# Loads of the opening stage on three queues, and the first high rows ahead of the second weight cast

## The chip, the cores and the metric

The kernel runs on one core of a Trainium2 chip. The metric is the device time of one execution in microseconds (us). Engines are named as in the profile: PE is TensorE (matmuls; PEld are its weight loads), DVE is VectorE, ACT is ScalarE, POOL is GpSimd, and SP is SyncE, which here only issues DMA transfers. A name with a q (SPq, ACTq, POOLq) is the queue of that engine, on which DMA issues and other instructions without data work stand.

## The reference

Two decoder layers over 256 tokens of width 1024, all in float32. What matters here is the first sub-layer's entry:

```python
mod = jax.nn.silu(c) @ w_ada + b_ada                 # c: (1, 1024), w_ada: (1024, 6144)
sh1, sc1, gt1, sh2, sc2, gt2 = jnp.split(mod, 6, axis=-1)
h = rms_norm(x, g_mix) * (1 + sc1[:, None, :]) + sh1[:, None, :]
proj = h @ w_in                                      # then two kinds of attention, gates, w_out
```

The layer then mixes the two attentions, adds the result to x, and runs a channel sub-layer (w_up, squared ReLU, w_down) behind a second norm of the same kind. Positions enter through rotary embedding of queries and keys.

## The kernel before

**Arithmetic.** Each float32 weight piece is split in two float32r parts, high and low: ACT casts the high part (`split_next`, L440) and DVE subtracts it for the low part (L446, or L961 in the opening stage). The activations are split the same way. A product is three matmuls (high by high, low by high, high by low).

**The opening stage** is `lead` (L881 to L1039). It is written out by hand: inside it each engine's instructions stand in exactly the order of the code, so a late instruction holds all that follow on its engine. Its order is as follows.

- `load_x` (L122) issues c and the two halves of x on SP, and on ACT's queue the positions, the rotary frequencies (`invf`) and the identity matrix (`ident`), the last two being columns of one tile, `cpack`. ACT's instructions wait behind these issues in its own order.
- `load_ada` loads four of sixteen pieces of the first w_ada columns; `ada_load` (L210) issues each piece as two transfers of 256 KB on SP. The four pieces of the first call, 0 to 3, hold the eight k rows of the shift and scale columns of the first two feature blocks, which is the first quarter, q = 0. Behind them stand the loads of w_in (`stream.load_next`, L418), then the next pieces.
- `silu_c` computes silu(c) on ACT and DVE. `load_rows` (L130) issues three small loads on ACT's queue behind it: the norm gains and the biases, as rows of one tile, `grow`. `rope_angles` (L343) puts some twenty small operations on DVE, which need the positions and `invf`.
- PE runs 24 wake matmuls on a tile of ones (L908).
- For each half t of x: ACT squares and sums (L926), DVE adds the two sums (L927), and POOL takes the power -1/2 (L928). POOL's earlier instructions are a few memsets. Between t = 0 and t = 1 stand the first two of eight weighted sums of the first quarter on DVE (`dve_sums`, L307, L313 and L315).
- ACT scales the rows of x by that power (`rows_scale`, L935), PE transposes them (L559, with `ident`), ACT copies the result (L939). PE transposes `grow` (L945), ACT copies it (`gcol`), PE runs eight more wakes. Then the second half of the columns: ACT scales both t (L935), PE transposes, DVE copies (L939), behind the last six weighted sums. PE turns the sums into columns (`columns`, L335).
- The quarter then passes the affine step (`apply`, L963): DVE adds biases and gains for shift `sh` and scale `s1` (L301, L304), ACT writes the high rows `hT_hi` of two feature blocks (L970, two instructions), DVE a full copy (L972) and the low rows (L975).
- Three casts of weights (`cast`, L956, which is `split_next` without the low part) serve the three groups of the product with w_in: queries, keys, values of the second attention (L977 on). In the kernel before two of the casts stand ahead of the first `apply`.
- The loop over q = 0 to 3 (L995) runs the product on PE quarter by quarter (`part`, L980, matmuls L984): the high by high matmuls of the three groups, then those with low parts. In between, PE sums the next quarter of w_ada (`pe_sums`, L325; for the last one DVE does it), `apply` prepares the next two feature blocks, and `cast` and `low` prepare the next weights. The 3 raw buffers of weights are refilled as they are read.

Eight semaphores take turns over the transfers of SP and ACT, so an issue also waits until an earlier transfer on its semaphore has landed; in the trace this shows as waits of SP's queue on transfers that have nothing to do with its own.

After the opening stage come the rest of the layer's product, attention, the mixing, the channel sub-layer and the second layer. None of their code is touched.

Of the kernel before, what the change touches and what calls it, by code (L numbers as in the profile page):

```python
# [15 lines left out]
P = 128  # L16
# [4 lines left out]
KT = D // P  # L21
HD = 64
HALF = HD // 2
# [55 lines left out]
def kernel(ctx: ExitStack, tc: tile.TileContext, io):  # L79
# [3 lines left out]
    nc = tc.nc  # L83
# [12 lines left out]
    def nm(s):  # L96
        cnt[s] = cnt.get(s, 0) + 1
        return f"{s}_{cnt[s]}"
# [7 lines left out]
    def ring(n, name):  # L106
        return work.tile([P, 512], F32, tag="ring", name=nm(name), bufs=RING)[:, :n]
# [3 lines left out]
    pos_i = const.tile([P, NT], I32, name="pos_i")  # L111
    cpack = const.tile([P, HALF + P + 4 * P], F32, name="cpack")
    invf = cpack[:, 0:HALF]
    ident = cpack[:, HALF:HALF + P]
    mask = cpack[:, HALF + P:]
    grow = ring(P, "grow")
# [5 lines left out]
    def load_x():  # L122
        nc.sync.dma_start(c8, io["c"][0].rearrange("(p k) -> p k", k=KT))
        for t in range(NT):
            nc.sync.dma_start(x_sb[:, t, :], io["x"][0, t * P:(t + 1) * P, :])
        nc.scalar.dma_start(pos_i, io["positions"][0].rearrange("(t p) -> p t", p=P))
        nc.scalar.dma_start(invf, io["cpack"][:, 0:HALF])
        nc.scalar.dma_start(ident, io["cpack"][:, HALF:HALF + P])

    def load_rows():  # L130
        nc.scalar.dma_start(grow[0:4 * KT, :], io["grow"])
        for l in range(DEPTH):
            o = (4 + 6 * l) * KT
            nc.scalar.dma_start(grow[o:o + 6 * KT, :], io["b_ada"][l].rearrange("(r c) -> r c", c=P))

    def load_gains():
        nc.sync.dma_start(gqk, io["gqk"][None].to_broadcast([P, DEPTH, 4, HD]))
# [20 lines left out]
    def silu_c():  # L158
        nc.scalar.activation(cs, ones[:, :KT], AF.Tanh)
        nc.scalar.activation(cs, c8, AF.Tanh, scale=0.5)  # L160
        nc.vector.scalar_tensor_tensor(out=cs, in0=cs, scalar=1.0, in1=c8, op0=ALU.add, op1=ALU.mult)
        nc.vector.tensor_scalar(out=cs, in0=cs, scalar1=0.5, scalar2=None, op0=ALU.mult)
        nc.vector.tensor_copy(cz[:, :, 0], cs)
# [46 lines left out]
    def ada_load(i):  # L210

        u, q = divmod(i, 4)
        if u >= len(ada_units) or i in ada_raw:
            return
        l, part, half = ada_units[u]
        col = part * D + half * 512
        src = io["w_ada"][l].rearrange("(p k) c -> p k c", k=KT)
        tag, o = room[i] if i < len(room) and room[i] else ("araw", 0)
        if tag == "araw":
            ada_raw[i] = araw.tile([P, 2, 512], F32, tag=tag, name=nm(tag))  # L220
        elif tag == "gt":
            ada_raw[i] = state.tile([P, D], F32, tag=tag, name=nm(tag), bufs=2).rearrange("p (k c) -> p k c", c=512)
        else:
            if o == 0:
                first[tag] = state.tile([P, 2, 2, 512], F32, tag=tag, name=nm(tag), bufs=1)
            ada_raw[i] = first[tag][:, o]
        if u < 4:
            for k in range(2):
                nc.sync.dma_start(
                    ada_raw[i][:, k, :].rearrange("p (a c) -> p a c", a=2),  # L230
                    src[:, 2 * q + k, 0:2 * D].rearrange("p (a c) -> p a c", a=2)[:, :, half * 256:half * 256 + 256])
        else:
            nc.sync.dma_start(ada_raw[i], src[:, 2 * q:2 * q + 2, col:col + 512])
# [8 lines left out]
    def ada_unit(u):  # L242
# [4 lines left out]
        for q in range(4):  # L247
            for a in range(ADA_BUFS if u > 3 else 0):
                ada_load(4 * u + q + a)
            raw = ada_raw[4 * u + q]  # L250
            if q == 2:
                bias_row(u + 1)
            for k in range(2):
                kk = 2 * q + k
                if kk == 0 and kind < 2:
                    nc.vector.tensor_scalar(out=acc, in0=raw[:, k, :], scalar1=cs[:, kk:kk + 1], scalar2=None,
                                            op0=ALU.mult)
                else:
                    nc.vector.scalar_tensor_tensor(  # L259
                        out=acc, in0=raw[:, k, :], scalar=cs[:, kk:kk + 1], in1=(bz if kk == 0 else acc),  # L260
                        op0=ALU.mult, op1=ALU.add)
                yield
# [34 lines left out]
    def ada_affine(l, sub, half, cols, n, kinds):  # L297
        for i, kind in enumerate(kinds):
            d = (sh if kind == 0 else s1)[l][sub][:, half * n:half * n + n]
            b = (4 + 6 * l + 3 * sub + kind) * KT + half * n  # L300
            nc.vector.tensor_tensor(out=d, in0=cols[:, i * n:i * n + n], in1=gcol[:, b:b + n], op=ALU.add)  # L301
            if kind == 1:
                g = (2 * l + sub) * KT + half * n
                nc.vector.scalar_tensor_tensor(out=d, in0=d, scalar=1.0, in1=gcol[:, g:g + n],  # L304
                                               op0=ALU.add, op1=ALU.mult)
# [25 lines left out]
    def columns(rows):  # L331

        ps = tmp_t()
        for i in range(4):
            nc.tensor.matmul(ps[:, i:i + 1], lhsT=rows[:, i * P:(i + 1) * P], rhs=ones[:, 0:1], start=True, stop=True,  # L335
                             skip_group_check=True)
        return ps
# [5 lines left out]
    def rope_angles():  # L343
        nc.vector.tensor_copy(pos_f, pos_i)
        ang = ring(NT * HALF, "ang").rearrange("p (t i) -> p t i", i=HALF)
        for t in range(NT):
            nc.vector.tensor_scalar(out=ang[:, t, :], in0=invf, scalar1=pos_f[:, t:t + 1], scalar2=None, op0=ALU.mult)
        ns = [ring(NT * HALF, "rtn").rearrange("p (t i) -> p t i", i=HALF) for _ in range(2)]
        for i in range(2):
            nc.vector.tensor_scalar(out=ns[i], in0=ang, scalar1=1.0 / (2.0 * math.pi), scalar2=0.25 * i,  # L350
                                    op0=ALU.mult, op1=ALU.add)
        for m in (MAGIC, -MAGIC):
            for i in range(2):
                nc.vector.tensor_scalar(out=ns[i], in0=ns[i], scalar1=m, scalar2=None, op0=ALU.add)
        for j, p in enumerate(TWO_PI_PARTS):
            for i in range(2):
                nc.vector.scalar_tensor_tensor(out=sincos[:, i], in0=ns[i], scalar=-p,
                                               in1=(ang if j == 0 else sincos[:, i]), op0=ALU.mult, op1=ALU.add)
        nc.vector.tensor_scalar(out=sincos[:, 1], in0=sincos[:, 1], scalar1=0.5 * math.pi, scalar2=None, op0=ALU.add)
        lim = 3.1415925  # L360
        nc.vector.tensor_scalar(out=sincos, in0=sincos, scalar1=lim, scalar2=-lim, op0=ALU.min, op1=ALU.max)
# [519 lines left out]
    def lead():  # L881
# [6 lines left out]
        def load_ada():  # L888
            for _ in range(4):
                ada_load(next(pieces))  # L890

        load_x()
        load_ada()
        stream.load_next()
        stream.between = load_ada
# [2 lines left out]
        load_ada()  # L898
        load_gains()
        silu_c()  # L900
        load_rows()
        rope_angles()

        wake_ps = tmp_t()
# [10 lines left out]
        r = [small.tile([P, 1], F32, tag="lnr", name=nm("lnr"), bufs=2) for _ in range(NT)]  # L915
# [38 lines left out]
        cols = columns(acc)  # L954

        def cast():  # L956
            stream.split_next("later")
# [5 lines left out]
        def apply(q, cols):  # L963

            ada_affine(0, 0, q, cols, 2, (0, 1))
            x = xnT[:, 2 * q:2 * q + 2, :]
            hf = ring(512, "hf").rearrange("p (j s) -> p j s", s=S)
            for i in range(2):
                j = 2 * q + i
                A.activation(hT_hi[:, j, :], x[:, i, :], AF.Identity, bias=sh[0][0][:, j:j + 1],  # L970
                             scale=s1[0][0][:, j:j + 1])
                V.tensor_scalar(out=hf[:, i, :], in0=x[:, i, :], scalar1=s1[0][0][:, j:j + 1],  # L972
                                scalar2=sh[0][0][:, j:j + 1], op0=ALU.mult, op1=ALU.add)
            js = slice(2 * q, 2 * q + 2)
            V.tensor_tensor(out=hT_lo[:, js, :], in0=hf, in1=hT_hi[:, js, :].bitcast(F32), op=ALU.subtract)  # L975
# [10 lines left out]


        cast()
        cast()
        apply(0, cols)  # L990
        cast()
        rope_sin()
        for _ in range(3):
# [1 line left out]
        for q in range(4):  # L995
# [21 lines left out]
            cols = columns(acc)  # L1017
# [23 lines left out]
    def mixing(l, rest, finish):  # L1041
# [6 lines left out]
        if l == 0:  # L1048
            with tc.manual_schedule():
                (qb, kb, vb), tabs = lead()  # L1050
        else:
            stream.retire(["qT", "kv"])
            tabs = rope_tables(l)
            qb = proj_first(rest, finish)
# [218 lines left out]
```

## Time and profile before

| | us |
|---|---|
| median of 3 runs | 757.29 (754.62 to 758.05) |
| profiled execution | 755.65 |
| its span in the trace | 753.9 |
| PE busy | 730.7 (97%) |
| DVE busy | 587.2 (78%) |
| ACT busy | 431.2 (57%) |
| POOL busy | 32.0 (4%) |

The span runs from the first to the last instruction; the rest of the execution's time lies around it. A row of a timeline gives the start, the duration, the engine, the line, the operation with output and inputs, how many instructions were merged (x8), and in brackets how long the engine had been idle and what released it. A row on a queue (ACTq) is the issue of a transfer, not the transfer. A chain of waits follows the end of the kernel back from each instruction to what released it. In time windows, busy times are us within the stretch, PEclk is the granted clock of TensorE as a share of full speed, and DMA is the mean busy share of the 16 DMA engines.

### The profile page before, as it was taken

Reading aid. Unit: us, or ns where it says so; the run is one execution under the profiler, and the core shown is the slowest. Engines: PE = TensorE matmul, PEld = TensorE weight load, DVE = VectorE, ACT = ScalarE, POOL = GpSimd, SP = SyncE. Lnnn points to the kernel's source line nnn. Section 1 sums busy time; section 2 is a strip of 40 time slices with the busy share of each in tenths; the row PEclk is TensorE's granted clock in tenths of the full one; section 3 lists DMA queues with packets and bytes.
Section 4 is the critical chain, followed back from the end, with each engine's and each line's share of the span. In section 5 each row is a group of like instructions: output and inputs, shape, how many; then the busy total and the mean of one; then the engine's idle time right before and its main releaser. Section 6 shows DMA issues by size and latency. Waiting matters only on the chain.

```text
span 753.9 us, 12320 instructions
## 1 busy us (share of the span) xinstructions
PE 730.7 (97%) x4713; PEld 645.3 (86%) x4713; DVE 587.2 (78%) x1090; ACT 431.2 (57%) x817; POOL 32.0 (4%) x24
## 2 busy tenths in 40 slices
PE   7999889999999999999999999999999999999997
PEld 6678778899778999989977888989988899999896
DVE  6598998999899988988789788987879745545542
ACT  6545579863466655455436357576447755555550
POOL 1003200000000000000000401000000000000000
PEclk9999999999999999999999999999999999999999
DMA  8996758877949999989882633844662865565501
GB/s 293 392 325 227 227 162 285 274 254 248 303 128 330 370 347 299 332 309 342 283 318 98 224 119 113 263 157 166 225 223 80 269 203 175 182 207 172 189 33 57
DMA packets 110538, 173.46 MB, mean 230 GB/s; under 512 B 4744, under 2 KB 68488, under 8 KB 110480
## 3 DMA queue, kind: packets, MB, share of 16 engines
q1 hardware_dynamic: 109744, 172.54, 67.9%
q8 instruction: 37, 0.61, 0.3%
q10 hardware_dynamic: 736, 0.15, 0.1%
q14 instruction: 21, 0.17, 0.1%
HBM read 171.62 MB, written 1.05 MB: 229 GB/s over the span
## 4 chain that ended last, share of the span: by engine, by line
PE 72%; DVE 13%; DMA 7%; ACT 3%; issue 2%; POOL 2%; SPq 0%; ACTq 0%; DVEq 0%; POOLq 0%
PE tmp L527 11%; PE acc L524 11%; PE acc L522 11%; PE acc L523 11%; PE tmp L528 10%; PE tmp L529 10%; DMA araw<-in_w_ada_dram 4%; DVE ada L259 2%; DVE w L446 2%; PE acc L984 2%; POOL rs L751 1%; ACT w L440 1%; PE tmp L870 1%; DMA wraw<-in_w_up_dram 1%; PE acc L810 1%
## 5 line engine op out<-in xcount | busy, mean ns | idle before, releaser
L446 DVE TENSOR_TENSOR w<-wraw,w 128x1024 fp32r<-128x1024 f32 x137 | 166.3, 1221 | 48.1 <-ACT w L440 46.8
L440 ACT CAST w<-wraw 128x1024 fp32r<-128x1024 f32 x150 | 155.9, 1048 | 78.9 <-PE acc L524 44.5
L527 PE MATMUL tmp<-hT_hi,w 128*128 128x256 f32 x480 | 140.1, 292 | 1.3 <-DVE alo L874 1.2
L529 PE MATMUL tmp<-hT_hi,w 128*128 128x256 f32 x480 | 135.9, 283 | 0.0
L528 PE MATMUL tmp<-hT_lo,w 128*128 128x256 f32 x480 | 135.7, 283 | 0.0
L259 DVE SCALAR_TENSOR_TENSOR ada<-araw,cs,ada 128x512 f32<-128x512 f32 x140 | 104.4, 746 | 3.2 <-DMA araw<-in_w_ada_dram 2.1
L527 PEld LDWEIGHTS tmp<-hT_hi,w 128*128 128x128 f32 x480 | 91.5, 191 | 8.2 <-issue 4.4
L528 PEld LDWEIGHTS tmp<-hT_lo,w 128*128 128x128 f32 x480 | 91.7, 191 | 0.7
L529 PEld LDWEIGHTS tmp<-hT_hi,w 128*128 128x128 f32 x480 | 91.6, 191 | 0.3 <-issue 0.3
L522 PE MATMUL acc<-w,uhi 128*128 128x512 f32 x192 | 75.4, 393 | 0.0
L523 PE MATMUL acc<-w,uhi 128*128 128x512 f32 x192 | 74.9, 390 | 0.0
L524 PE MATMUL acc<-w,ulo 128*128 128x512 f32 x192 | 74.9, 390 | 0.0
L1164 ACT ACTIVATE relu<-tmp 128x256 f32<-128x256 f32 x56 | 21.5, 384 | 68.8 <-PE tmp L529 68.8
L524 PEld LDWEIGHTS acc<-w,ulo 128*128 128x128 f32 x192 | 36.1, 188 | 7.6
L522 PEld LDWEIGHTS acc<-w,uhi 128*128 128x128 f32 x192 | 36.1, 188 | 6.9
L523 PEld LDWEIGHTS acc<-w,uhi 128*128 128x128 f32 x192 | 36.1, 188 | 6.8
L440 ACT CAST kv<-wraw 128x1024 fp32r<-128x1024 f32 x21 | 22.1, 1051 | 24.6 <-PE acc L524 19.8
L446 DVE TENSOR_TENSOR ahi<-wraw,ahi 128x1024 fp32r<-128x1024 f32 x18 | 22.0, 1222 | 15.0 <-ACT ahi L440 14.9
L446 DVE TENSOR_TENSOR kv<-wraw,kv 128x1024 fp32r<-128x1024 f32 x21 | 25.7, 1222 | 9.9 <-ACT kv L440 9.8
L446 DVE TENSOR_TENSOR qT<-wraw,qT 128x1024 fp32r<-128x1024 f32 x21 | 25.6, 1220 | 8.3 <-ACT qT L440 8.3
L527 PE MATMUL tmp<-hT_hi,alo 128*128 128x256 f32 x112 | 31.8, 284 | 0.0
L528 PE MATMUL tmp<-hT_lo,alo 128*128 128x256 f32 x112 | 31.7, 283 | 0.0
(248 smaller groups left out, 1744.8 us busy)
## 6 DMA issues: line engine op xcount, KB each, us to landing
araw<-in_w_ada_dram SPq DMA_DIRECT2D x80, 512.0 KB, 5.9
wraw<-in_w_up_dram SPq DMA_DIRECT2D x32, 1024.0 KB, 5.9
wraw<-in_w_down_dram SPq DMA_DIRECT2D x32, 1024.0 KB, 5.9
wraw<-in_w_in_dram SPq DMA_DIRECT2D x28, 1024.0 KB, 5.7
wraw<-in_w_out_dram SPq DMA_DIRECT2D x8, 1024.0 KB, 5.6
wraw<-in_w_in_dram SPq DMA_DIRECT2D x12, 512.0 KB, 7.1
wraw<-in_w_o_swa_dram SPq DMA_DIRECT2D x8, 512.0 KB, 3.3
wraw<-in_w_o_moba_dram SPq DMA_DIRECT2D x8, 512.0 KB, 5.1
```

The lines of the kernel that those rows point to most:

```text
L259: nc.vector.scalar_tensor_tensor(out=acc, in0=raw[:, k, :], scalar=cs[:, kk:kk + 1], in1=(bz if kk == 0 else acc), op0=ALU.mult, op1=ALU.add)
L440: nc.scalar.copy(hi, r)
L446: ins = nc.vector.tensor_tensor(out=lo, in0=r, in1=hi.bitcast(F32), op=ALU.subtract)
L522: nc.tensor.matmul(ps, lhsT=lh, rhs=rh, start=start, stop=False)
L523: nc.tensor.matmul(ps, lhsT=lh, rhs=rl, start=False, stop=False)
L524: nc.tensor.matmul(ps, lhsT=ll, rhs=rh, start=False, stop=stop)
L527: nc.tensor.matmul(ps, lhsT=wh, rhs=ah, start=start, stop=False)
L528: nc.tensor.matmul(ps, lhsT=wh, rhs=al, start=False, stop=False)
L529: nc.tensor.matmul(ps, lhsT=wl, rhs=ah, start=False, stop=stop)
L751: nc.gpsimd.tensor_tensor(out=rs, in0=ss, in1=mhalf[:, :NT * nh].rearrange("p (t h) -> p t h", h=nh), op=ALU.pow)
L984: T.matmul(ps[t], lhsT=left[:, 2 * q + k, t * P:(t + 1) * P], rhs=w[:, k, :], start=(first and k == 0), stop=(last and k == 1))
L1164: nc.scalar.activation(r, ps, AF.Relu)
```

## The change

Three edits, all in the opening stage. The pieces 1 and 3 of the first quarter of w_ada, two transfers each, are issued on ACT's queue instead of SP's, where they stand first in ACT's order. The six small loads (positions, frequencies, identity, and the three of `load_rows`) are issued on POOL's queue instead of ACT's, and `load_rows` is called right behind `load_x`, so that all six stand ahead of POOL's first power; the memsets stay ahead of them. And the first `apply` stands behind one cast of weights instead of two.

```diff
         for t in range(NT):
             nc.sync.dma_start(x_sb[:, t, :], io["x"][0, t * P:(t + 1) * P, :])
-        nc.scalar.dma_start(pos_i, io["positions"][0].rearrange("(t p) -> p t", p=P))
-        nc.scalar.dma_start(invf, io["cpack"][:, 0:HALF])
-        nc.scalar.dma_start(ident, io["cpack"][:, HALF:HALF + P])
+        nc.gpsimd.dma_start(pos_i, io["positions"][0].rearrange("(t p) -> p t", p=P))
+        nc.gpsimd.dma_start(invf, io["cpack"][:, 0:HALF])
+        nc.gpsimd.dma_start(ident, io["cpack"][:, HALF:HALF + P])
 
     def load_rows():
-        nc.scalar.dma_start(grow[0:4 * KT, :], io["grow"])
+        nc.gpsimd.dma_start(grow[0:4 * KT, :], io["grow"])
         for l in range(DEPTH):
             o = (4 + 6 * l) * KT
-            nc.scalar.dma_start(grow[o:o + 6 * KT, :], io["b_ada"][l].rearrange("(r c) -> r c", c=P))
+            nc.gpsimd.dma_start(grow[o:o + 6 * KT, :], io["b_ada"][l].rearrange("(r c) -> r c", c=P))
...
             for k in range(2):
-                nc.sync.dma_start(
+                (nc.scalar if i in (1, 3) else nc.sync).dma_start(
                     ada_raw[i][:, k, :].rearrange("p (a c) -> p a c", a=2),
...
         load_x()
+        load_rows()
         load_ada()
...
         silu_c()
-        load_rows()
         rope_angles()
...
         cast()
+        apply(0, cols)
         cast()
-        apply(0, cols)
         cast()
```

## Rows read from the trace of the kernel before

**Rows 1.** Time windows, last stretch; columns: busy us of each engine, granted clock, DMA.

```profile
60.40:753.90 693.50, 676.55 (x4425) 602.52 (x4423) 543.93 (x996) 397.84 (x766) 29.16 (x14) 1.00 0.66 221
```

**Rows 2.** Chain of waits in order of time, 0 to 60 us; columns: start, us, what.

```profile
7.66 5.03 DMA araw<-in_w_ada_dram
...
12.78 0.76 DVE aq L315
...
16.64 0.17 DVE s L304
```

**Rows 3.** Timeline of ACT, 0 to 45 us; columns: start, us, what, idle before and releaser.

```profile
3.78 0.34 ACTq L131 DMA_DIRECT2D grow<-in_grow_dram  x1
...
5.24 0.63 ACT L926 ACTIVATE ln<-x_sb 128x512 f32<-128x512 f32 x1 [1.26 <-DMA x_sb<-in_x_dram]
...
11.15 0.72 ACT L935 ACTIVATE ln<-x_sb,lnr 128x512 f32<-128x512 f32 x1 [1.21 <-POOL lnr L928]
...
13.31 1.35 ACT L935 ACTIVATE ln<-x_sb,lnr 128x512 f32<-128x512 f32 x2
...
15.41 1.04 ACT L440 CAST w<-wraw 128x1024 fp32r<-128x1024 f32 x1 [0.75 <-DMA wraw<-in_w_in_dram]
16.69 1.04 ACT L440 CAST w<-wraw 128x1024 fp32r<-128x1024 f32 x1 [0.24 <-DMA wraw<-in_w_in_dram]
17.64 1.09 ACT L970 ACTIVATE hT_hi<-ln,sh,s 128x256 fp32r<-128x256 f32 x2
...
35.57 1.05 ACT L440 CAST w<-wraw 128x1024 fp32r<-128x1024 f32 x1 [4.29 <-DMA wraw<-in_w_in_dram]
```

**Rows 4.** Timeline of PE, 0 to 58 us.

```profile
0.99 8.40 PE L908 MATMUL tmp<-ones 128*128 128x128 f32 x48 [0.99 <-POOL mhalf L148]
...
18.29 2.15 PE L984 MATMUL acc<-w,hT_hi 128*128 128x512 f32 x8 [2.02 <-ACT hT_hi L970]
20.27 1.07 PE L984 MATMUL tmp<-w,hT_hi 128*128 128x512 f32 x4
...
42.56 2.14 PE L984 MATMUL acc<-w,hT_hi 128*128 128x512 f32 x8 [1.14 <-ACT hT_hi L970]
```

**Rows 5.** Timeline of DVE, 0 to 20 us.

```profile
5.49 0.39 DVE L347 TENSOR_SCALAR ang<-cpack,pos_f 128x32 f32<-128x32 f32 x2 [0.76 <-DMA cpack<-in_cpack_dram]
...
8.04 0.23 DVE L361 TENSOR_SCALAR sincos<-sincos 128x128 f32<-128x128 f32 x1
...
16.38 0.16 DVE L301 TENSOR_TENSOR sh<-tmp,gcol 128x2 f32<-128x2 f32 x1
```

**Rows 6.** Timeline of POOL, 0 to 62 us.

```profile
1.38 0.31 POOL L156 MEMSET cz<- 128x256 f32 x1
8.54 0.65 POOL L928 TENSOR_TENSOR lnr<-lnr,mhalf 128x1 f32<-128x1 f32 x1 [6.84 <-DVE lnr L927]
10.12 0.99 POOL L928 TENSOR_TENSOR lnr<-lnr,mhalf 128x1 f32<-128x1 f32 x1 [0.93 <-DVE lnr L927]
```

**Rows 7.** All instructions of line 928; columns: count, min/median/max ns, first and last start.

```profile
L928 POOLq MODIFY_POOL_CONFIG  x2: 11/11/11, 1.6 to 1.7; - x2
L928 POOL TENSOR_TENSOR lnr<-lnr,mhalf x2: 654/824/995, 8.5 to 10.1; 128x1 f32<-128x1 f32 x2
```

**Rows 8.** DMA issues, 0 to 62 us: the small cpack load of ACT's queue.

```profile
cpack<-in_cpack_dram ACTq DMA_DIRECT2D x1, 16.0 KB, 4.2
```

**Rows 9.** Waits of SP's queue, 0 to 62 us; columns: us in total, times, longest.

```profile
SPq L229 <- DMA cpack<-in_cpack_dram: 3.3, 2, 2.9
```

**Rows 10.** Time windows of all engines, two stretches of loads.

```profile
6.50:13.50 7.00, 5.12 (x42) 4.70 (x42) 5.97 (x20) 4.20 (x12) 1.65 (x2) 1.00 0.92 287
...
20.00:48.00 28.00, 26.75 (x138) 18.75 (x138) 19.77 (x40) 13.56 (x18) 0.00 (x0) 1.00 1.07 390
```

**Rows 11.** Time windows of line 908 alone (wake matmuls), two single microseconds.

```profile
3.00:4.00 1.00, 1.00 (x7) 1.00 (x6) 1.00 0.92 361
8.00:9.00 1.00, 1.00 (x11) 1.00 (x10) 1.00 0.97 335
```

## The prediction

> **What bounds the kernel now.** I read the time windows first. From 60.4 us to the end PE is busy 676.55 of 693.50 us [rows 1]: none of the moved instructions lies there, and there is little idle time in which a late start could vanish. So the change acts in the first 60 us, and what the product with w_in gains or loses there reaches the end almost one for one. The chain of waits tells what comes before that product: a w_ada transfer is awaited until 12.69, the last three weighted sums run from 12.78 to about 15.1, and the scale s of the first two feature blocks is done at 16.81 (16.64 + 0.17) [rows 2]. The timeline of ACT shows the rest [rows 3]: the high rows (L970) start at 17.64 and not right behind s, because the second weight cast (16.69 to 17.73, itself behind its transfer) stands ahead of them. PE then starts at 18.29 after 2.02 us idle, begins its third group at 20.27, and waits once more for high rows, 1.14 us, ahead of 42.56 [rows 4]. DVE's table of angles (rope_angles) runs from 5.49, when its frequencies land, to 8.27, ahead of all sums; the affine step starts at 16.38 [rows 5].
>
> **POOL's queue, which I hold to decide.** Today POOL clears its last tile by 1.69 and then does nothing until its first power (L928) at 8.54 [rows 6]. But line 928 also shows two MODIFY_POOL_CONFIG at 1.6 and 1.7, 11 ns each [rows 7]: the power needs something set up, and the 6.85 us up to 8.54 hide whatever that takes, while POOL is listed as waiting for DVE. In the changed kernel six loads (positions, frequencies, identity, three of the grow rows) stand in POOL's queue in program order ahead of line 928. No row shows a load issued by POOL. From below an issue costs 0.34 us, the shortest on ACT's queue [rows 3]; from above 0.99, the longer of line 928's two one-element powers; I take 0.82, the middle of the two [rows 7], because both are work of POOL on almost no data. Six are 4.94 us (2.0 to 6.0): the configuration passes at 6.63 instead of 1.69. What it takes then is bounded by 0 and 6.85 us; I take the upper end, since that stretch is the only one in the trace in which it ran at all, and nothing on POOL begins inside it. The first power then starts at 13.48 and takes 0.65, and the second ends at 13.48 + 0.65 + 0.99 = 15.12, instead of 11.11 (10.12 + 0.99) [rows 6]: 4.01 us late. The Trainium skill (GPSIMD Engine Reference, 2.1 Instruction dispatch) says that the first call of a freshly loaded POOL kernel pays about 6 us, measured as 5.95 from MODIFY_POOL_CONFIG, with no visible instruction. By that figure the sum below would be 0.9 us lower; the trace of before fits it, with 6.85 us of room, and does not show it.
>
> **What follows from the late power.** The second scaling of rows (L935) starts 0.04 us after it, at 15.16 instead of 11.15 [rows 3]. From there to the end of L935's last pair (13.31 + 1.35 = 14.66) ACT and PE work in turn on each other's results, 3.51 us, and to the affine step (16.38) another 1.72 [rows 3, 5]: transposes, copies, column sums. So the pair ends at 18.67, the affine step starts at 20.39, and s is there at 20.82. The sums on DVE are done before they are needed: the frequencies, second on POOL, are issued at 2.51 and land 4.2 us later, as they do today [rows 8]; the table ends 2.78 us after that, by 9.5, and eight sums of at most 0.76 us end at 15.6, four microseconds ahead of the column sums. If that cover is gone, they bind: second rival.
>
> **The high rows ahead of the second cast.** ACT does the first cast behind the last scaling, 18.67 to 19.75, and the high rows right behind s at 20.85. The first matmul follows 0.65 later as today, at 21.50, which is 3.2 us late. But the order only exchanges: the second and third cast now stand behind 1.09 us of high rows and take 2 x 1.04 us [rows 3], so the third group starts at 20.85 + 1.09 + 2.08 + 0.03 = 24.05 instead of 20.27. PE's order is fixed, so 3.78 us is what the product is late. Taken alone, the edit gives the first group 0.83 us (17.64 - 16.81) and takes most of it back at the third.
>
> **Loads.** SP loses four issues and the 3.3 us for which its w_ada issues wait on the cpack loads of ACT's queue [rows 9]. ACT gets four issues for six, each 0.3 to 0.5 us, and the four all stand ahead of its table load: that and the tanh move by some tenths, hidden by the 1.26 us for which ACT waits for x today [rows 3]; without that wait the tenths would count. The new loads share the DMA engines with x, so x lands later, by at most the 1 MB put beside it, 2.7 us at 390 GB/s: ACT's squares would start at 7.9 instead of 5.24 and still have 5.6 us until the first power. Identity and grow rows are read by PE after 14.9, later than today, and POOL has issued all six by 6.63. From 6.5 to 13.5 the DMA engines move 287 GB/s, and 390 later [rows 10]: with a fuller queue that stretch gives back up to 7 x (1 - 287/390) = 1.8 us, and all of w_in's loads come up to that much sooner. On the path this is worth the following: ACT's cast at 35.57 waits 4.29 us for its transfer [rows 3], DVE's low part, tables and sums come behind it, and the 1.14 us idle of PE ahead of 42.56 is their end. With the transfers sooner and PE 3.8 us later that idle time goes; next late there is PE itself, busy to 41.42.
>
> **Sum.** 3.78 - 1.14 = 2.64 us late. The profiled execution took 755.65 us (span 753.9, the rest around it), so 758.3; it lies 1.64 under the median of the runs, 757.29, so against that 759.9. Bounds: issues at 0.34 or 0.99 us move it by -2.9 or +1.0, the configuration by down to -6.85, until other things bind (second rival).
>
> **Rivals.** First, slower: TensorE's clock falls. Today the longest idle stretch of PE that a row shows is the 2.02 us, and every window is granted 1.00, that is 2.4 GHz. In the forecast PE has nothing between its wake matmuls (end 9.39) [rows 4] and its first transposes, at 14.9 (first power done at 14.13, then 0.04 and 0.72 for ACT's scaling): 5.5 us. The wakes ran 7 to a microsecond from 3 to 4 us and 11 from 8 to 9 [rows 11], though both rows say 1.00; I read the first rate as the level of 1.2 GHz. If the clock falls in the gap and the next 6 us of work (the first rise lay between 4 and 8 us) run at that rate, it costs 6 x (1 - 7/11) = 2.2 us: +4.8 us, 762.1. It decides as soon as POOL is late enough for the gap; against it speaks that transposes, second wakes and column sums come before the product and take part of the slow time where PE waits anyway. The Trainium skill (TensorE: Matmul & The Clock Gate, Part 1) says that an idle array goes back to half its clock; no idle stretch of before is long enough to agree or not. Second, the configuration costs nothing that shows, or does not stand behind the loads: then the sums on DVE bind, 15.6 instead of 15.1, s is there at 17.3, the third group starts at 17.33 + 3.2 = 20.53, 0.3 late, and with the 1.14 us back it is 0.8 faster: 756.5. Third, POOL's small loads also land no later than today and the w_ada loads sooner: sums from 8.27 without a wait end at 14.4, s is there at 16.1, the third group at 19.3, 1.0 sooner, and with the 1.14 it is 2.1 faster: 755.2. Against it speaks that x and the first pair of w_ada share the engines with what ACT issues before them.
>
> **How the numbers follow.** 0.5% is 3.8 us, about what a measurement of this kernel can tell from no change. Forecast 0.42, first rival 0.28, second 0.18, third 0.12. Slower by over 0.5%: nearly all of the first rival and the forecast's upper end (+3.7 at 0.99 us an issue), 0.32. Faster by over 0.5% would need 3.8 us, more than the third rival has: 0.04 for what I do not see. The rest, 0.64, is no change. The range goes from 755.4, just above the third rival, to 764.0, the first rival with issues of 0.99 us (763.1) and a microsecond for the runs.
>
> **What would show it.** Line 928: configuration behind six issues of POOL at about 6.6, first power near 13.5, second scaling near 15.2. High rows near 20.9 with one cast ahead, first product matmul near 21.5, third group near 24. No idle PE where the 1.14 us were. The SP waits on cpack gone, 6.5 to 13.5 us above 287 GB/s. A first power before 9 us is the second or third rival; a granted clock under 1.00, or matmuls of twice the length, ahead of the third group is the first. A time under 755 us would mean that I have missed what the loads held up.

## The result, and the profile after

| | before | after |
|---|---|---|
| median of the runs, us | 756.89 (754.62 to 758.05) | 765.79 (765.36 to 766.32) |
| profiled execution, its span, us | 755.65, 753.9 | 765.57, 763.8 |
| mean granted clock of the profiled execution | 1.000 | 0.987 |

The ratio is 1.0117, interval 1.0091 to 1.0143: slower by 8.9 us, or 1.2%. A second set of runs (last experiment) gave 1.0086 (1.0060 to 1.0113), 6.3 us: a loss of 6 to 9 us. The forecast was 759.9 us, no change, with 764.0 as its upper end.

The timeline of ACT, 0 to 30 us, of the changed kernel (columns as in [rows 3]):

```profile
0.74 0.99 ACTq L229 DMA_DIRECT2D araw<-in_w_ada_dram  x2
2.93 4.62 ACTq L229 DMA_DIRECT2D ahi<-in_w_ada_dram  x2
7.58 1.28 ACT L159 ACT_TABLE_LOAD   x1 [7.58 <-DMA x_sb<-in_x_dram]
...
9.11 0.21 ACT L160 ACTIVATE cs<-c 128x8 f32<-128x8 f32 x1
9.23 0.61 ACT L926 ACTIVATE ln<-x_sb 128x512 f32<-128x512 f32 x1
...
15.42 0.72 ACT L935 ACTIVATE ln<-x_sb,lnr 128x512 f32<-128x512 f32 x1 [0.84 <-POOL lnr L928]
...
19.27 1.05 ACT L440 CAST w<-wraw 128x1024 fp32r<-128x1024 f32 x1
23.05 1.09 ACT L970 ACTIVATE hT_hi<-ln,sh,s 128x256 fp32r<-128x256 f32 x2 [2.73 <-DVE s L304]
24.05 1.98 ACT L440 CAST w<-wraw 128x1024 fp32r<-128x1024 f32 x2
```

Read the first three rows as one. The two issues of piece 1 take 0.99 us. The two of piece 3 take 4.62 us, and ACT's first instruction of any work, the table load, follows them at 7.58 with x named as what ended the wait. Each issue by itself is short (0.37 us in the trace); the second of this pair stood until 7.17, when the second half of x had landed. The squares (L926), at 5.24 before [rows 3], start at 9.23, and the high rows (L970) at 23.05 instead of 17.64.

The timeline of DVE, 0 to 24 us:

```profile
9.36 0.17 DVE L161 SCALAR_TENSOR_TENSOR cs<-cs,c 128x8 f32<-128x8 f32 x1 [9.36 <-DMA ahi<-in_w_ada_dram]
...
10.11 0.39 DVE L347 TENSOR_SCALAR ang<-cpack,pos_f 128x32 f32<-128x32 f32 x2
...
12.79 0.21 DVE L927 TENSOR_SCALAR lnr<-lnv 128x1 f32<-128x1 f32 x1
12.92 0.47 DVE L313 TENSOR_SCALAR aq<-araw,cs 128x512 f32<-128x512 f32 x1
...
21.24 1.29 DVE L939 COPY ln<-tmp 128x512 f32<-128x512 f32 x2 [2.34 <-PE tmp L559]
22.54 0.16 DVE L301 TENSOR_TENSOR sh<-tmp,gcol 128x2 f32<-128x2 f32 x1
```

The first row names a w_ada transfer as its releaser, but cs waits for the tanh, which ends at 9.32 on ACT: the transfer is only what came last by the profile. Behind cs stand the table of angles (10.11, before 5.49 [rows 5]) and behind that the sum of squares L927 at 12.79, for which POOL waits. The affine step starts at 22.54 instead of 16.38.

All instructions of line 928, and, in a second view, the loads on POOL's queue (size, and median us from issue to landing):

```profile
L928 POOLq MODIFY_POOL_CONFIG  x2: 33/35/37, 5.2 to 5.2; - x2
L928 POOL TENSOR_TENSOR lnr<-lnr,mhalf x2: 663/830/998, 13.2 to 14.4; 128x1 f32<-128x1 f32 x2
...
  DVE lnr L927: 8.6, 2
```

```profile
cpack<-in_cpack_dram POOLq DMA_DIRECT2D x1, 64.0 KB, 6.6
grow<-in_b_ada_dram POOLq DMA_DIRECT2D x2, 24.0 KB, 6.3
pos_i<-in_positions_dram POOLq DMA_DIRECT2D x1, 1.0 KB, 7.1
cpack<-in_cpack_dram POOLq DMA_DIRECT2D x1, 16.0 KB, 6.6
```

POOL has passed its configuration at 5.2 and starts the power at 13.2, released by DVE. The frequencies (the 16 KB load) land 6.6 us after their issue, not 4.2 [rows 8].

The timeline of PE, 0 to 30 us, and the row at which 42.56 stood before [rows 4]:

```profile
1.00 8.38 PE L908 MATMUL tmp<-ones 128*128 128x128 f32 x48 [1.00 <-POOL mhalf L148]
14.63 1.11 PE L559 MATMUL tmp<-cpack,ln 128*128 128x128 f32 x4 [5.25 <-ACT ln L935]
...
17.31 3.46 PE L908 MATMUL tmp<-ones 128*128 128x128 f32 x16
20.60 1.04 PE L559 MATMUL tmp<-cpack,ln 128*128 128x128 f32 x8
...
23.70 3.65 PE L984 MATMUL acc<-w,hT_hi 128*128 128x512 f32 x8 [1.27 <-ACT hT_hi L970]
27.15 1.16 PE L984 MATMUL tmp<-w,hT_hi 128*128 128x512 f32 x4
...
48.53 1.69 PE L984 MATMUL acc<-w,hT_hi 128*128 128x512 f32 x6
```

PE is idle for 5.25 us, the first eight matmuls of the product then take 3.65 us instead of 2.15, the third group is 6.88 us late, and the 1.14 us of idle time are gone: 5.97 us are left at the end of the opening stage. Time windows (columns as in [rows 1]) show the clock, and two later stretches in which it fell again:

```profile
6.50:13.50 7.00, 2.88 (x24) 2.69 (x23) 3.83 (x25) 4.15 (x11) 0.34 (x1) 1.00 1.02 322
13.50:20.00 6.50, 4.92 (x22) 4.52 (x23) 5.23 (x8) 4.57 (x9) 1.32 (x2) 0.51 1.07 391
...
149.00:153.00 4.00, 3.43 (x20) 3.10 (x20) 3.73 (x12) 4.00 (x14) 0.00 (x0) 0.65 0.81 268
217.00:222.00 5.00, 4.43 (x14) 2.98 (x13) 4.88 (x15) 2.56 (x8) 0.67 (x1) 0.66 0.38 120
```

From 13.5 to 20 us the granted clock is 0.51, close to the lower of the two levels, 1.2 GHz. From 24 to 27 us, under the product's first matmuls, it is 0.50 again.

### The profile page after: what moved, and what is told of

It reads as the page before. It is cut to its first block, busy times and chain, and to the rows that moved or that the text cites. A ratio compares the mean times of both kernels' runs of the same rounds, so it can differ in the third digit from the quotient of the medians.

```text
span 763.8 us, 12326 instructions
## 1 busy us (share of the span) xinstructions
PE 737.7 (97%) x4713; PEld 650.6 (85%) x4713; DVE 587.1 (77%) x1090; ACT 430.6 (56%) x817; POOL 34.6 (5%) x30
## 4 chain that ended last, share of the span: by engine, by line
PE 65%; DVE 19%; DMA 7%; ACT 3%; issue 3%; POOL 2%; SPq 0%; ACTq 0%; DVEq 0%; POOLq 0%
PE acc L522 10%; PE acc L524 10%; PE acc L523 10%; PE tmp L527 9%; PE tmp L529 9%; PE tmp L528 9%; DVE w L446 4%; DVE ada L259 3%; DMA araw<-in_w_ada_dram 3%; PE acc L984 3%; POOL rs L751 2%; DMA wraw<-in_w_o_moba_dram 1%; PE tmp L984 1%; DMA wraw<-in_w_up_dram 1%; DVE rb L771 1%
## 5 line engine op out<-in xcount | busy, mean ns | idle before, releaser
L527 PE MATMUL tmp<-hT_hi,alo 128*128 128x256 f32 x112 | 31.8, 284 | 0.0
L529 PE MATMUL tmp<-hT_hi,alo 128*128 128x256 f32 x112 | 31.7, 283 | 0.0
```

Source lines behind the costliest of these rows:

```text
L527: nc.tensor.matmul(ps, lhsT=wh, rhs=ah, start=start, stop=False)
L529: nc.tensor.matmul(ps, lhsT=wl, rhs=ah, start=False, stop=stop)
```

## The experiments

Three theories stood against each other. **W**: ACT's last two w_ada issues wait, and hold ACT's work. **S**: the small loads land late from POOL's queue, and hold DVE's table of angles. **C**, the forecast's own: POOL's configuration delays the power. The table has the third product group's start from each profile (20.27 before [rows 4]; 27.15 after), the median and the ratio to before.

| kernel | third group | us | ratio, interval |
|---|---|---|---|
| small loads on POOL alone | 25.73 | 761.59 | 1.0060 (1.0041 to 1.0080) |
| w_ada pieces on ACT alone | 27.36 | 761.80 | 1.0075 (1.0048 to 1.0103) |
| order of casts alone | 22.24 | 757.40 | 1.0006 (0.9991 to 1.0022) |
| after, 44 first wakes | 28.38 | 766.02 | 1.0114 (1.0095 to 1.0132) |
| after, one piece on ACT | 25.98 | 761.13 | 1.0051 (1.0030 to 1.0071) |
| the same, angles later | 24.93 | 763.47 | 1.0089 (1.0063 to 1.0116) |
| before, grow rows on POOL | 20.15 | 756.06 | 0.9973 (0.9955 to 0.9991) |
| before, no first wakes | 20.63 | 756.19 | 0.9988 (0.9968 to 1.0008) |
| grow rows and order of casts | 21.70 | 756.64 | 0.9989 (0.9971 to 1.0007) |
| after, no second wakes | 27.94 | 764.12 | 1.0082 (1.0054 to 1.0111) |
| grow rows, no second wakes | 21.93 | 756.81 | 0.9998 (0.9979 to 1.0018) |
| grow rows again | 18.88 | 756.87 | 0.9989 (0.9968 to 1.0011) |
| before, 28 second wakes | 24.45 | 759.42 | 1.0035 (1.0007 to 1.0063) |
| after again | 26.53 | 763.78 | 1.0086 (1.0060 to 1.0113) |
| one piece on ACT, again | 24.66 | 763.02 | 1.0081 (1.0051 to 1.0111) |

**The three parts, each alone.** First the six small loads: the kernel before with

```diff
-        nc.scalar.dma_start(pos_i, io["positions"][0].rearrange("(t p) -> p t", p=P))
+        nc.gpsimd.dma_start(pos_i, io["positions"][0].rearrange("(t p) -> p t", p=P))
...
         load_x()
+        load_rows()
         load_ada()
```

(and the other five likewise).

> The kernel before with one part of the change: the six small loads on POOL's queue, load_rows behind load_x. W_ada stays on SP, the first apply stays behind two casts. Theory W (the fourth w_ada issue on ACT's queue waits for x and holds tanh, squares and all of DVE): this part alone is nearly free, the angle table starts within 1 us of 5.5, the first power within 1 us of 8.5, time 756 to 758.5. Theory S (small loads issued by POOL land late): positions and frequencies land near 9, the table starts near 9.2, the first power near 12.3, the first product matmul near 22, PE's clock falls in the gap ahead of it, time 762 to 765. Theory C (POOL's configuration behind the loads, as forecast): the first power waits though the sums of squares are there, POOL's idle time is not put down to DVE.

The timeline of DVE in this run, and the one of POOL:

```profile
8.55 0.39 DVE L347 TENSOR_SCALAR ang<-cpack,pos_f 128x32 f32<-128x32 f32 x2 [0.25 <-DMA cpack<-in_cpack_dram]
```

```profile
11.60 0.66 POOL L928 TENSOR_TENSOR lnr<-lnr,mhalf 128x1 f32<-128x1 f32 x1 [6.45 <-DVE lnr L927]
```

ACT's squares were on time, at 4.71. The table of angles waited for its frequencies until 8.55 and the power for DVE. S holds by itself, and costs 4.3 us by the medians (761.59, just under the 762 to 765 expected).

That the loads land late is shown; what makes them late is not. A part of it can be POOL's queue: 16 KB of grow rows issued at 3.78 on ACT's queue landed 3.8 us later in the kernel before, and issued at 3.63 on POOL's queue 7.0 us later here. But the bulk beside them changed too. In the kernel before, SP's first six w_ada issues stood on the cpack loads among others; here they did not, and went out in half the time:

```profile
2.11 6.02 SPq L229 DMA_DIRECT2D araw<-in_w_ada_dram  x6
```

```profile
2.12 3.04 SPq L229 DMA_DIRECT2D araw<-in_w_ada_dram  x6
```

The first row is SP's timeline before, the second that of this run. In the run with only the grow rows on POOL (below) these landed 5.1 and 5.3 us after their issue, between the two. No run here moves one of the two alone.

Then the pieces on ACT:

```diff
-                nc.sync.dma_start(
+                (nc.scalar if i in (1, 3) else nc.sync).dma_start(
```

> The kernel before with one part of the change: pieces 1 and 3 of w_ada on ACT's queue, behind the three small loads that stay there. Theory W: an issue among them waits until x has landed, the table load of ACT starts near 7.5, tanh near 9, the sums of squares near 9.3, the first power near 12 to 13, time 762 to 765. Theory S: without POOL's loads ACT and DVE keep today's times within 1 us, time 756 to 758.5.

The timeline of ACT in this run:

```profile
4.92 2.29 ACTq L229 DMA_DIRECT2D ahi<-in_w_ada_dram  x2
7.24 1.28 ACT L159 ACT_TABLE_LOAD   x1 [7.24 <-DMA x_sb<-in_x_dram]
...
9.99 1.51 ACTq L134 DMA_DIRECT2D grow<-in_b_ada_dram  x2
11.55 0.63 ACT L926 ACTIVATE ln<-x_sb 128x512 f32<-128x512 f32 x1 [2.56 <-DMA araw<-in_w_ada_dram]
```

W holds by itself too, with 4.5 us by the medians (761.80, again just under the range): ACT's work begins at 7.24, and the grow loads wait in their turn ahead of the squares. Each of the two alone makes the opening nearly as late as both, since they hold the same instruction by two roads: with both, cs is there at 9.36 (W) and the frequencies at about 9.1 (S: issue 2.54, 6.6 us on). That is why they don't add up in the opening. Last the order:

```diff
         cast()
+        apply(0, cols)
         cast()
-        apply(0, cols)
         cast()
```

> The kernel before with the first apply ahead of the second cast and nothing else. By the forecast the edit only exchanges: the first matmul near 17.5 instead of 18.29, the third group within 0.4 of 20.27, time within 1 us of the kernel before (756 to 758). Rival: the earlier start is kept, 0.8 us faster.

No difference in time. The starts that were expected did not come: the first matmul ran at 18.94 and the third group 2 us late, with the first eight matmuls at 3.51 us, since TensorE's clock fell there with every load as before. So falls of the clock in the opening are nothing that only the change brings.

**More first wakes**, to close PE's gap in the changed kernel (`WAKE = (24, 8)` to `(44, 8)`).

> The changed kernel with 44 wake matmuls instead of 24, so that PE has work until about 14.3, just ahead of its first transposes at 14.6. Theory K (the clock that falls in PE's gap of 5.25 us costs): granted clock 1.00 up to the product, second wakes 2.0 instead of 3.46 us, first eight product matmuls 2.15 instead of 3.65, time 761 to 763.5. Rival (ACT and DVE bind there anyway): within 1 us of 765.8.

Nothing gained, and no clean test: in this execution ACT's table load came at 8.73, so PE was still idle for 2.79 us, and the second wakes took 3.62 us, slow again.

**One piece on ACT.** `i in (1, 3)` becomes `i == 1`.

> The changed kernel with only piece 1 on ACT's queue, two issues, so that none of them has to wait for an earlier transfer. If the wait of ACT's last two issues is one of the two causes and the late landing of POOL's small loads the other: ACT's table load near 1.8 us, squares near 5 to 7, rope_angles still near 8.6, first power near 11.7, and a time like that of the run with the small loads alone on POOL, 760 to 762.5 us. If it is the sharing of the DMA engines by three queues that delays things, and not the wait in ACT's order: squares still past 8.5 us and 764 to 766 us.

```profile
0.74 0.98 ACTq L229 DMA_DIRECT2D araw<-in_w_ada_dram  x2
1.75 1.28 ACT L159 ACT_TABLE_LOAD   x1 [1.75 <-issue]
...
5.12 0.63 ACT L926 ACTIVATE ln<-x_sb 128x512 f32<-128x512 f32 x1 [1.62 <-DMA x_sb<-in_x_dram]
...
8.49 0.63 ACT L926 ACTIVATE ln<-x_sb 128x512 f32<-128x512 f32 x1 [2.04 <-DMA x_sb<-in_x_dram]
```

This is ACT's timeline there. With two issues nothing waits, the table load is at 1.75, and what is left is S: the angles at 8.92, the time of the first run. The last row shows a smaller price: the second half of x came at 8.49, where it held nothing up before. Which of the loads put beside it did that is not separated.

**The angles out of the way**: the same, with `rope_angles()` moved behind the second L927, so that only POOL's own queue stands ahead of the first power.

> The changed kernel with only piece 1 on ACT and with rope_angles moved on DVE behind the second L927, so that neither cause stands ahead of the powers any more; what is left ahead of the first power is POOL's own queue. If the configuration takes 6 to 6.85 us behind POOL's six issues (passed at about 5.2): first power at 11.2 to 12.0, second scaling near 13.5, affine step near 19, 760 to 762 us. If the configuration costs little: first power near 6.7 to 7.5, no clock fall ahead of the product, the sums on DVE then end last, near 16.5 (1.4 later than before, with rope_angles in between), affine step near 17.8, 757.5 to 759.5 us.

All instructions of the power, one line higher in this kernel:

```profile
L927 POOLq MODIFY_POOL_CONFIG  x2: 33/35/37, 5.2 to 5.2; - x2
L927 POOL TENSOR_TENSOR lnr<-lnr,mhalf x2: 553/558/562, 6.9 to 11.5; 128x1 f32<-128x1 f32 x2
```

C falls: the power starts at 6.91, at most 1.7 us behind the configuration and 0.37 us after the start of the DVE instruction (6.54) that releases it. The rest of the expectation failed. The affine step came at 20.18 and not near 17.8, the product's first eight matmuls took 3.78 us, and the time is no better than that of the run with one piece on ACT. The first weighted sum tells one reason:

```profile
9.64 0.48 DVE L313 TENSOR_SCALAR aq<-araw,cs 128x512 f32<-128x512 f32 x1 [2.88 <-DMA araw<-in_w_ada_dram]
```

That row of DVE's timeline ran at 8.30 in the kernel before. The first piece came later, not sooner, and the angles now stand between the sums. That the spread over two queues made it late is not shown: in the run with the small loads alone, with w_ada wholly on SP, a transfer of the first piece also landed only at 9.7.

**Only what is needed late on POOL**: the kernel before with the three grow loads on POOL's queue, early.

> The kernel before with only the three late-needed loads (gains and biases, the grow rows) on POOL's queue, early; positions, frequencies and identity stay on ACT's. If late landing hurts only what is needed early: rope_angles at 5.5 as before, grow rows there by 10, ahead of their transpose near 12.6, first power at 8.5, time 756 to 757.5 us, no slower than before. If POOL's configuration takes the 6.85 us of my prediction and stands behind the three issues (near 3.4 us): first power near 10.2, second scaling 1.7 late, time 758.5 to 760 us.

Angles at 5.20, power at 8.26, the six later sums without a wait from 9.32 on. About 2 us faster in this set of runs; 1.2 us by the medians of another (below), whose interval includes 1.

**The clock by itself**: the kernel before without first wakes, `WAKE = (0, 8)`.

> The kernel before without its 24 first wake matmuls (the eight second ones stay), nothing else: the price of a low TensorE clock in the opening by itself, with every load where it was. If the clock is part of the loss: PE starts at about 11.9 at the low level, second wakes near 3.5 us instead of 1.95, the product's first eight matmuls near 3.5 instead of 2.15, time 759 to 761 us (1.5 for the second wakes, 1 to 2 for the product). If PE's slow time falls where PE waits anyway: 757 to 758 us.

PE's timeline there:

```profile
9.71 1.12 PE L559 MATMUL tmp<-cpack,ln 128*128 128x128 f32 x4 [9.71 <-DMA araw<-in_w_ada_dram]
...
12.36 2.85 PE L908 MATMUL tmp<-ones 128*128 128x128 f32 x16
...
18.64 2.15 PE L984 MATMUL acc<-w,hT_hi 128*128 128x512 f32 x8 [1.77 <-ACT hT_hi L970]
```

Transposes and second wakes ran slowly, the product at full rate, and the time is that of before, under both ranges that were expected. Here the low clock ahead of the product cost nothing, as other work ended later: the high rows stood behind a second cast that waited for its transfer, and DVE waited only 0.30 us for PE. To cost time it would have to reach the product, or PE would have to be what is late.

**Two harmless parts, second wakes, and the grow rows again.** One set of four: the grow rows on POOL with the new order of casts; the changed kernel with `WAKE = (24, 0)`; the grow rows with `WAKE = (24, 0)`; the grow rows once more.

> Two parts of the change that cost nothing in its own trace: only the grow rows on POOL's queue, early, and the first high rows ahead of the second cast; w_ada wholly on SP, positions, frequencies and identity on ACT. If both causes are out of the way and the order edit is worth nothing, as its run alone showed: the time of the run with the grow rows alone on POOL, about 2 us under before, 755 to 757 us. If the order edit gains now that the sums end sooner (casts no longer behind their transfers): 0.3 to 0.8 us less than that run. A version that should beat both kernels.

> The changed kernel without its eight second wake matmuls. In the changed kernel they took 3.46 us at the low clock instead of 1.95 and stand ahead of PE's second transposes, for which DVE waits 2.34 us. If the low clock's price lies there: DVE's L939 waits little, s and the high rows come some 2 us sooner (high rows near 21), 762.5 to 764.5 us. If the low clock's price lies in the product's first matmuls, or the product starts colder without them: first eight matmuls 3.6 to 4.3 us, the gain is given back, 765 to 767 us.

> The kernel with only the grow rows on POOL, early, without the eight second wake matmuls. There DVE's L939 waited 1.70 us for PE behind second wakes of 2.82 us. If PE is what ends last ahead of the affine step: s near 15.8 instead of 17.2, product from about 17, 754 to 755.5 us. If the product then starts at the low clock (first eight matmuls near 3.5 instead of 2.14): 756 to 757.5 us, nothing gained.

> The kernel with only the grow rows on POOL's queue, once more, beside its two variants. If its gain is real: 1 to 3 us under before, ratio 0.996 to 0.999. If the earlier figure came from which runs fell in the pairs: ratio 0.999 to 1.001.

None of the three with the grow rows can be told from before by its interval. With the new order of casts, and without second wakes, the product started at the low clock (3.50 and 3.78 us for its first eight matmuls). The changed kernel without second wakes (1.0082) lies under the first set of the changed kernel (1.0117) but not clearly under its second (1.0086), and in its profile the clock stays low right through the first groups, so a gain is not shown:

```profile
11.00:28.00 17.00, 9.55 (x34) 7.89 (x35) 14.05 (x39) 10.72 (x21) 1.66 (x2) 0.51 1.07 392
```

The grow rows' two profiles are of one program: second wakes 2.82 us in one and 1.95 in the other, product from 18.17 and from 16.89, and yet the sooner one ended later (span 754.5 against 751.8). Where the clock falls differs from execution to execution.

**A known shift, and the two kernels side by side.** Open was how 6 us at the end of the opening became 8.9, and why one piece less on ACT gave nearly 5 us where the openings differ by about 1. The first kernel is the one before with `WAKE = (24, 28)`.

> The kernel before with 28 second wakes instead of 8, every load where it was: 20 more wakes at 1.95/8 us each make PE's second transposes about 4.9 us later, less the half microsecond or so that PE had to spare, with PE busy so that its clock has no reason to fall. If a shift of the opening passes one for one behind it: high rows near 22, product +4.4, the 1.14 us idle gone, 3.3 us over before, 760.5 to 761.5 us. If something behind the opening grows with a shift: over 762.5 us. If the rest absorbs it: under 759.5 us.

> The changed kernel once more, beside the next one. Ratio 1.010 to 1.013, 765 to 767 us. If ACT's wait for the second half of x varies from execution to execution: table load between 7.5 and 8.8 us in this profile, first product matmul between 23.5 and 25.

> The changed kernel with only piece 1 on ACT, once more, beside the changed kernel. If the wait on ACT's queue costs what the medians said: 4 to 5 us under the changed kernel, 760.5 to 762 us. If it costs what the two openings showed (1.1 us): 763.5 to 765.5 us.

PE's timeline in the first:

```profile
11.96 7.57 PE L908 MATMUL tmp<-ones 128*128 128x128 f32 x56
19.36 1.04 PE L559 MATMUL tmp<-cpack,ln 128*128 128x128 f32 x8
22.47 2.15 PE L984 MATMUL acc<-w,hT_hi 128*128 128x512 f32 x8 [1.28 <-ACT hT_hi L970]
```

The product is 4.18 us late and 3.15 at the row that stood at 42.56, the idle time taken off; the span is 3.7 longer than that of before. In this profile the shift passes about one for one. The median is 2.0 us over before, by the ratio 2.7 (0.5 to 4.8): 759.42 lies just under the 759.5 below which the rest was to have absorbed it, and the interval is too wide to tell passing from half absorbing or from a growth to 4.8. The second execution profiled of the changed kernel has ACT's wait longer, and the clock at full for the product (ACT's timeline, then PE's):

```profile
3.13 5.33 ACTq L229 DMA_DIRECT2D ahi<-in_w_ada_dram  x2
8.49 1.28 ACT L159 ACT_TABLE_LOAD   x1 [8.49 <-DMA x_sb<-in_x_dram]
```

```profile
24.07 1.23 PE L984 MATMUL acc<-w,hT_hi 128*128 128x512 f32 x4 [1.28 <-ACT hT_hi L970]
25.50 1.20 PE L984 MATMUL acc<-w,hT_hi 128*128 128x512 f32 x4 [0.20 <-ACT w L440]
26.53 1.11 PE L984 MATMUL tmp<-w,hT_hi 128*128 128x512 f32 x4
```

The changed kernel came out faster than expected (1.0086 and 763.78, not 1.010 and 765). Side by side the two differ by 0.8 us, less than either interval, while their openings differ by 1.1 us in the first profiles and 1.9 in these (third group 26.53 and 24.66). The second median with one piece, 763.02, lies between the two ranges that were expected. So the 5 us between the earlier medians can't be taken for the wait's price.

## Why the prediction was wrong, point by point

The step that failed is the one held to decide: that POOL's configuration keeps the first power waiting for 6.85 us. It takes at most 1.7. What kept the power waiting were two terms taken as nearly unchanged: the issues ahead of ACT's table load (some tenths forecast, 5.3 us measured) and the landing of the frequencies (4.2 us as before, 6.6 measured). And the sum left TensorE's clock to a rival; I put it at 2.8 us below.

The direction was right, and so was the place of the larger part: 5.97 us of loss arise in the first 50 us, where the forecast said 2.64, and the 1.14 us of idle time were given back.

| step, us | forecast | measured |
|---|---|---|
| POOL's six issues, configuration passed at | 6.63 | 5.2 |
| first power starts | 13.48 | 13.16 |
| second power ends | 15.12 | 15.38 |
| second scaling to affine step | 5.23 | 7.12 |
| affine step to third group | 3.66 | 4.61 |
| third group late | 3.78 | 6.88 |

- **The cause of the late power was wrong, its size right by accident.** The run with the angles moved shows at most 1.7 us of configuration where the forecast took 6.85. The power was late because DVE's L927 was, and that this made the end of the second power 4.27 us late, against 4.01 forecast, is luck. The Trainium skill (GPSIMD Engine Reference, 2.1 Instruction dispatch) gives 5.95 us from MODIFY_POOL_CONFIG for a first call of a freshly loaded kernel. No run here shows them; the power at 6.91 is 1.7 us behind it. An issue on POOL took 0.50 to 0.89 us, within the bounds, and 0.59 in the mean of the six against the 0.82 taken.
- **"That and the tanh move by some tenths" was the step that failed on ACT.** The table load moved by 5.3 us, from 2.24 in the trace of before to 7.58. The rule was in the description of the kernel: eight semaphores take turns, and an issue waits for the earlier transfer on its own. c, two halves of x and eight w_ada transfers are eleven, so three must wait, and two of them had been put on ACT: the first stood until c was there (2.93), the second until the second half of x was (7.17). With piece 3 back on SP it is SP that waits for x there, 3.6 us, and ACT's table load starts at 1.75. I counted SP's 3.3 us [rows 9] as removed and did not ask whose queue waits next.
- **"Land 4.2 us later, as they do today" was the step that failed on DVE.** From POOL's queue, next to more of x and w_ada at once, it was 6.6 us. The sums' cover of four microseconds was gone with it; the sums themselves were not late, their start was.
- **The first rival's mechanism came true as well**, in a forecast that had kept it apart: PE was idle 5.25 us (forecast 5.5), and the clock fell. Of the 6.88 us, 1.89 are the longer way from second scaling to affine step (second wakes 3.46 instead of 1.95, for which DVE waits 2.34) and 0.95 the product's first matmuls. With 0.26 for the later power these make the 3.10 by which the forecast fell short in the opening. I put the first two, 2.8, down to the clock, where the rival had 2.2; no run changes the clock alone in this kernel, but where it was at full the same stretches were as short as forecast: 5.11 us from second scaling to affine step in the second profile of the grow rows, 3.63 from affine step to third group in the second of the changed kernel. The Trainium skill (TensorE: Matmul & The Clock Gate, Part 1) says that an idle array goes back to half its clock. 0.51 behind 5.25 us of idle time agrees. With the order of casts alone the clock also fell, and there the pauses of PE ahead of it were at most 1.40 us. In the second profile of the changed kernel, with the product at full clock, the third group is 6.26 late, although ACT worked 0.9 later.
- **The order of casts** changed nothing in the time, as said: 1.0006. That it exchanges the first group for the third, its own profile can't show, as the clock fell there; in the second profile of the changed kernel PE waits 0.20 us for a cast within the first groups. **SP's waits on cpack** were gone and 6.5 to 13.5 us moved 322 GB/s instead of 287 [rows 10], but the sums did not start before 12.92, so nothing came of it.
- **Behind the opening**, the forecast had nothing. The profiled execution of after loses another 3.9 us there (9.9 of span less 5.97), the second one 3.5; the windows at 149 and 217 us show part of it. But the profiled execution of before is the odd one: its clock was 1.000, other runs of before show 0.987 to 1.000 (most 0.990 to 0.995), and their median is 1.2 to 2.5 us over it. Each of the sixteen other profiles, with the early loads moved or not, has one to three stretches at the low level behind 60 us, and that of before none; the second of the grow rows has two, like both of after (0.66 from 77 to 82 us and from 207 to 212). So part of the 3.9 us is not the change's. Not all of it is explained by that: against the same profile of before, the seven profiles of kernels that leave w_ada, positions and frequencies where they were lose -1.3 to 2.2 us behind the opening. What of the loss there belongs to the change stays open. The second set's 6.3 us (4.5 to 8.6) have room for the opening's 5.3 to 6.0 alone, the first set's 8.9 (6.9 to 10.8) do not.

## What to carry to other kernels

Before a transfer goes to the queue of an engine that also computes, count the transfers ahead of it against the semaphores they share: an issue that has to wait holds everything behind it on that engine, so only issues that need not wait belong there. A queue that stands idle was fit here for what is needed late (the grow rows), not for what is needed first (the frequencies); ask of each small load who reads it and when. Taking waits away from a queue of bulk loads, as from SP's here, puts more of them beside the small ones. And of a single profile, compare the clock before comparing the ends.

## What the runs showed that I had not expected

Small loads from POOL's queue landed 6.3 to 7.1 us after their issue beside the big loads, and 5.8 to 7.0 in the kernel with that part alone. Two causes that each made the opening 5 to 6.4 us late made it 5.3 to 6.0 late together, as both hold one instruction. The clock falls in single stretches behind the opening, at other places in each execution, in every profile but that of before: the same program gave spans of 751.8 and 754.5 us. And 24 wake matmuls at the start were worth nothing that could be measured (0.9988, 0.9968 to 1.0008).
